# A DeltaNet and dilated-attention layer on one core: bias table from 128 partitions, new buffers for the second half, and last loads re-placed

## The chip, the core and the metric

The kernel runs on one core of a Trainium2 chip. The metric is the device time of one execution in microseconds; lower is better. Three executions of the kernel before took 1434.2, 1432.68 and 1436.26 us, with a median of 1434.2.

## The reference

One layer for a sequence of 2048 positions of width 1024, in float32:

```python
h = rms_norm(x, norm_w)
proj = h @ w_in                       # 1024 -> 4104 columns: q, k, v, z, b, a of DeltaNet; q, k, v, gate of attention
# gated DeltaNet: 4 heads of 128, chunks of 64
q, k, v = split(silu(causal_conv4(qkv_dn)));  q, k = l2_norm(q), l2_norm(k)
for each chunk:                       # u, w from a triangular solve within the chunk
    v_new = u - w @ S;  o = q_dec @ S + attn_intra @ v_new
    S = S * g_last + k_tail.T @ v_new
y_dn = rms_norm(o, dn_norm_w) * silu(z)
# attention: 8 heads of 64, three patterns (window, dilation) = (128,1), (512,4), (2048,16)
for each pattern:
    scores = q @ k_window.T + bias[t5_bucket(step * dilation)]   # causal band of 129 keys
    o_p, lse_p = softmax(scores) @ v_window, logsumexp(scores)
y_att = sum(softmax over patterns(lse_p) * o_p) * silu(gate)
out = x + concat(y_dn, y_att) @ w_out
```

## The kernel before

All products of the projections and of the output run as three TensorE matmuls on rounded parts (high by high, high by low, low by high), so every operand x, weight or mixed activation is first "split": ACT copies the high part (xh, wh, mhh), DVE subtracts to get the low part (xl, wl, mhl). The work falls into stages that PE runs through in this order.

1. Projections of DeltaNet's q, k, v with their convolution, of z and the gates, and the inverse of the 32x32 diagonal blocks of the triangular systems, which DVE computes row by row. This is some 450 us. Their end also builds the bias table: `pb` is one matmul of the 33 rows of `rel_bias` with a one-hot table, and lines 594 f. write it to memory as `bs_d`, 64 copies of a row of 256 values per head and pattern, so that attention can load it as a sheared band.
2. The delta rule, up to about 801 us. `stage2` (line 606) prepares four chunks of a pair of heads: it loads kT, qT, vT (transposed k, q and v), Qr, E (decays), TTz and D0t (parts of the triangular system) on SP's queue and makes at, Ks and U from them. `chain` runs the recurrence of a chunk. `dn_out` (line 741) loads the gate rows zs, norms and gates the result and stores it as `y_d`. A scheduler orders these three by priorities. Products of attention's projections (`proj_fill`, tile pj) fill PE between them: 960 are free to go, what is beyond is held until the delta rule's last PE operation.
3. Attention. From here on every instruction is issued as written: `Queue` (line 88) chains each engine's instructions in program order, and all of them show line 99. The outputs are in two halves of 1024 positions, each with four pairs of heads. A pair of heads takes 12 steps, so there are 96 (and a few before and behind). `step` calls `scores` (sc, scores of a unit; DVE adds the bias and takes the maximum ml, ACT the exponential pr), `turned` (pt, transposes of pr, copied to pT) and `values` (pv, the product with V), and between them takes filler matmuls: in steps -4 to 47 `proj_fill`, 9, 9 and 8 of them; in steps 48 to 97 `out_fill`, 4, 4 and 3.
4. `at_step` is the table that puts the rest into a step's three places (0, 1, 2): `load` (q, K and the bias of a pair, 4 steps ahead), `queries`, `keys`, `vload`, `sums`, `weigh` and `weigh2` (weights of the three patterns), `blend_load` (weights as Fb, gate as gt), `blend` (on POOL, one per quarter of the positions) and `mixed` (the store to `mx_d`).
5. `out_fill` computes out = x + mixed @ w_out in rows of 128 positions. A job is a row's "dn" half (yt, loaded from `y_d`, turned by PE) or its "att" half (mt, loaded from `mx_d`). `half_load` loads it, `half_split` splits it, `products` yields the matmuls (tile po), and res, loaded from x or from a partial sum, takes the result. w_out is split by `wo_split`: its first four blocks of 128 rows near the end of `proj_fill` (loads `w_out_load`, tile wraw), the other four inside `out_fill` (RAW).
6. Behind step 97 the last pair is weighed, blended on DVE and multiplied (`opening`, `closing`).

DMAs are issued from SP's queue unless the code says `adma` (ACT's). SP and ACT share eight completion lanes: a DMA waits for the DMA eight back on its lane.

Of the kernel before, what the change touches and what calls it, by code (L numbers as in the profile page):

```python
# [84 lines left out]
def hybrid(tc, xT, x, norm_w, w_in, conv_w, a_log, dt_bias, dn_norm_w, q_norm_w, k_norm_w,  # L85
# [53 lines left out]
    bs_d = dr.tile([8, 3, 64 * 256], F32, name="bs_d")  # L139
# [447 lines left out]
    bv = scr[:8, :768].rearrange("p (a b) -> p a b", a=3)  # L587
    for i in range(2):
        pb = psA.tile([P, 512], F32, name="pm", bufs=1)
        n = 512 - 256 * i  # L590
        nc.tensor.matmul(pb[:8, :n], rb, oh[:, i * 512:i * 512 + n], start=True, stop=True)
        nc.vector.tensor_copy(scr[:8, i * 512:i * 512 + n], pb[:8, :n])
# [13 lines left out]
    def stage2(pair, c0):  # L606
# [15 lines left out]
        for s_ in range(2):  # L622
            dma(Qr[:, :, s_], dap(rows_d, (12 + 2 * pair + s_) * S + c0 * CH, [[0, P], [CH, 4], [1, CH]]))
# [5 lines left out]
        dma(E, Es_d[hf][pair, cc:cc + 4].rearrange("u p i -> p u i"))  # L629
# [3 lines left out]
        for s_ in range(2):  # L633
            a = s_ * CH
            dma(TT[a:a + CH, :, a:a + CH], A_d[hf][pair, cc:cc + 4, a:a + CH].rearrange("u p i -> p u i"))
            dma(D0[a:a + 32], dap(D0_d[hf], (m0 + s_) * 1024, [[32, 32], [2048, 4], [1, 32]]))
# [66 lines left out]
        return dict(WQ=WQ, at=at_, Ks=Ks, U=U, o4=o4)  # L703
# [54 lines left out]

# [9 lines left out]
    G = {}  # L768
    for p_ in range(2):
        G[p_] = at_prio("prep", stage2, p_, 0)  # L770
    for c0 in range(0, 32, 4):
# [8 lines left out]
        for p_ in range(2):  # L780
            at_prio("out", dn_out, p_, c0, cur[p_])
# [83 lines left out]
    def wo_split(kt, raw):  # L865
        wh, wl = W[kt]
        if kt < 4:
            nc.scalar.mul(wh, raw, dnw)
            nc.vector.scalar_tensor_tensor(wl, raw, dnw, wh.bitcast(F32), op0=ALU.mult, op1=ALU.subtract)
# [11 lines left out]
    def w_out_load(k):  # L881
        r = wp.tile([P, 4, 260], F32, name="wraw", bufs=2).rearrange("p a b -> p (a b)")[:, :1024]
        dma(r, w_out[k * P:(k + 1) * P, :])
        return r

    def proj_fill():
# [5 lines left out]
        for s_ in range(12):  # L892
# [3 lines left out]
            for o8 in range(8):  # L896
# [70 lines left out]
    def heads(hf, p):  # L967
# [5 lines left out]
        def load():  # L973
            g["q1"] = at0.tile([P, 1024], F32, name="q1", bufs=QB)
            g["k1"] = KC[p % 2] if hf else K0[:, p % 2 * 1024:(p % 2 + 1) * 1024]
            dma(g["q1"], qkT_d[0][p][:, T0:T0 + 1024])
            dma(g["k1"], qkT_d[1][p][:, :1024 * (hf + 1)])
            g["bias"] = bias = at0.tile([P, 3, 192], F32, name="bias", bufs=2)
            for s_ in range(2):
                dma(bias[s_ * CH:(s_ + 1) * CH],  # L980
                    dap(bs_d, (2 * p + s_) * 3 * 64 * 256 + 63, [[255, CH], [64 * 256, 3], [1, 192]]))
# [222 lines left out]
        g.update(load=load, keys=keys, queries=queries, vload=vload, scores=scores, turned=turned, values=values,  # L1204
# [13 lines left out]
    G[0]["load"]()  # L1218
    take(gen, 2 * 192)
# [24 lines left out]
    for i, g in enumerate(G):  # L1244
        b = 12 * i
        if i:
            at_step(b - 4, 1, g["load"])
        at_step(b - (2 if i else 3), 1, g["queries"], 0)
# [11 lines left out]
        if i < 7:  # L1260
# [5 lines left out]
            for qd in range(4):  # L1266
                d = i < 6
                at_step(b + 16 + qd + d, 0 if d else 2, g["blend_load"], qd)
                at_step(b + 17 + qd + d, 0 if d else 1, g["blend"], qd, nc.gpsimd)
                at_step(b + 19 + qd + d, 0 if d else 1, g["mixed"], qd)  # L1270
# [254 lines left out]
```

## Time and profile before

| | us |
|---|---|
| median of three executions | 1434.2 (1432.68 to 1436.26) |
| profiled execution | 1434.53 |
| its span | 1432.6 |
| mean granted TensorE clock | 0.988 |
| PE busy | 1376.4, 10262 matmuls |
| DVE, ACT, POOL busy | 905.4, 677.1, 438.4 |
| DMA | 205.00 MB, mean 143 GB/s |

The span is from the first to the last instruction of the trace; the time of the execution has a little around it. "Busy" counts the time in which an engine has an instruction in work. The waits view lists for how long an engine stood idle and what came last before it went on. The windows view gives busy time, granted clock (PEclk, 1.00 is full speed) and the DMA engines' mean busy share for stretches of the span.

### The profile page before, as it was taken

The page shows a single profiled execution, that of the slowest core. Times are in us where ns is not written, and L with a number is a line of the kernel's source. Part 1 is how long each engine was busy: PE and PEld are TensorE (multiplying, and loading weights), DVE is VectorE, ACT ScalarE, POOL GpSimd, SP SyncE. Part 2 cuts the span into 40 slices and gives each one's busy share as a digit, 9 for nine tenths or more (in the row PEclk, how much of TensorE's full clock was granted, in tenths as well). Part 3 has the DMA queues.
Part 4 walks back from the last instruction along what each step waited for, and adds up shares of the span by engine and source line. Part 5 has one row for each costly group of instructions (what it writes and reads, how often), then busy time and mean ns, then how long its engine had stood idle before and what let it go on. Part 6 is the DMA issues. An engine that isn't in the chain of part 4 may idle for free.

```text
span 1432.6 us, 28797 instructions
## 1 busy us (share of the span) xinstructions
PE 1376.4 (96%) x10262; PEld 1224.8 (85%) x10262; DVE 905.4 (63%) x2787; ACT 677.1 (47%) x1929; POOL 438.4 (31%) x507
## 2 busy tenths in 40 slices
PE   8999999999999997999999899999998989999998
PEld 7998777777777797999999889999997778888877
DVE  7535668799995365777777664634444645556465
ACT  5634436652221333444444376666565545555520
POOL 3000000000002113442332523565675275665500
PEclk9999999999999999999999999999999999999999
DMA  6563446763648646557553555274657474765664
GB/s 192 179 111 83 101 89 136 150 121 84 116 77 176 171 80 165 134 147 193 129 147 77 114 132 137 76 190 98 147 135 235 138 253 135 220 169 158 194 191 142
DMA packets 301154, 205.00 MB, mean 143 GB/s; under 512 B 149283, under 2 KB 271027, under 8 KB 300500
## 3 DMA queue, kind: packets, MB, share of 16 engines
q1 hardware_dynamic: 233924, 171.70, 48.6%
q10 hardware_dynamic: 67088, 31.47, 8.0%
q8 instruction: 81, 1.33, 0.4%
q14 instruction: 61, 0.50, 0.1%
HBM read 142.61 MB, written 60.50 MB: 142 GB/s over the span
## 4 chain that ended last, share of the span: by engine, by line
PE 66%; DVE 14%; DMA 9%; ACT 4%; issue 4%; SPq 1%; POOL 1%; ACTq 0%; DVEq 0%; POOLq 0%
PE pj L99 15%; PE po L99 9%; PE sc L99 6%; PE pz L99 5%; PE pv L99 4%; PE pj L206 4%; PE pj L207 4%; PE pj L208 4%; PE pt L99 4%; DVE cy L478 3%; DVE inv L545 2%; DMA kT<-cv 2%; PE C L719 2%; PE SU L725 2%; DVE inv L547 2%
## 5 line engine op out<-in xcount | busy, mean ns | idle before, releaser
L99 ACT ACTIVATE pr<-pr,ml 128x192 f32<-128x192 f32 (+2 forms) x384 | 156.8, 409 | 168.7 <-DVE ml L99 156.9
L99 PE MATMUL pj<-wh,xh 128*128 128x256 f32 (+1 forms) x776 | 228.2, 294 | 3.6 <-DVE t L99 2.3
L99 PE MATMUL pj<-wl,xh 128*128 128x256 f32 (+1 forms) x776 | 226.6, 292 | 0.0
L99 PE MATMUL pj<-wh,xl 128*128 128x256 f32 (+1 forms) x776 | 224.9, 290 | 0.0
L208 PE MATMUL pj<-xh,wl 128*128 128x512 f32 x512 | 203.6, 398 | 3.2 <-DVE wl L192 3.2
L206 PE MATMUL pj<-xh,wh 128*128 128x512 f32 x512 | 203.8, 398 | 1.4 <-ACT cy L480 1.2
L207 PE MATMUL pj<-xl,wh 128*128 128x512 f32 x512 | 203.0, 396 | 0.0
L99 PEld LDWEIGHTS pj<-wh,xh 128*128 128x128 f32 x776 | 147.6, 190 | 4.3 <-DVE t L99 2.7
L99 PEld LDWEIGHTS pj<-wl,xh 128*128 128x128 f32 x776 | 148.0, 191 | 0.6 <-issue 0.4
L99 PEld LDWEIGHTS pj<-wh,xl 128*128 128x128 f32 x776 | 147.7, 190 | 0.2
L99 DVE CUSTOM_DVE_ANT_0 pr<-sc,bias 128x192 f32<-128x192 f32 (+2 forms) x384 | 100.3, 307 | 74.3 <-PE sc L99 73.4
L208 PEld LDWEIGHTS pj<-xh,wl 128*128 128x128 f32 x512 | 96.5, 188 | 26.6 <-DVE wl L192 4.5
L206 PEld LDWEIGHTS pj<-xh,wh 128*128 128x128 f32 x512 | 96.6, 189 | 24.8 <-ACT cy L480 1.6
L478 DVE SCALAR_TENSOR_TENSOR cy<-cu,cw,cy 128x512 f32<-128x512 f32 x144 | 107.6, 749 | 15.9 <-ACT cy L476 14.4
L207 PEld LDWEIGHTS pj<-xl,wh 128*128 128x128 f32 x512 | 96.5, 188 | 22.0
L99 POOL COPY qz<-q 64x512 f32<-64x512 f32 x96 | 94.5, 984 | 57.8 <-PE sc L99 53.9
L662 POOL MEMSET at__4536<- 64x256 f32 x1 | 0.3, 306 | 354.5 <-PE pj L207 354.5
L99 DVE COPY pT<-pt 64x128 f32<-64x128 f32 (+2 forms) x220 | 69.4, 323 | 60.1 <-PE pt L99 56.8
L99 PE MATMUL po<-xh,mhh 128*128 128x512 f32 x212 | 89.6, 422 | 2.5 <-ACT mhh L99 2.5
L99 POOL TENSOR_TENSOR Fb<-Fb,op 128x256 f32<-128x256 f32 x84 | 70.6, 854 | 60.8 <-DMA Fb<-F 59.7
L99 PE MATMUL po<-xl,mhh 128*128 128x512 f32 x212 | 88.6, 418 | 0.0
L99 PE MATMUL po<-xh,mhl 128*128 128x512 f32 x212 | 88.4, 417 | 0.0
(365 smaller groups left out, 3169.8 us busy)
## 6 DMA issues: line engine op xcount, KB each, us to landing
wraw<-in_w_in SPq DMA_DIRECT2D x44, 512.0 KB, 7.0
cv<-cy ACTq DMA_DIRECT2D x48, 256.0 KB, 2.6
Fb<-F SPq DMA_DIRECT2D x64, 192.0 KB, 5.8
xr<-in_xT SPq DMA_DIRECT2D x32, 256.0 KB, 4.1
kT<-cv SPq DMA_DIRECT2D x32, 256.0 KB, 3.3
qk<-qs ACTq DMA_DIRECT2D x64, 128.0 KB, 3.6
res<-in_x SPq DMA_DIRECT2D x13, 512.0 KB, 5.3
V<-v_d SPq DMA_DIRECT2D x20, 256.0 KB, 6.2
```

Of the source, the lines that this page charges most:

```text
L99: i = f(*args, **kw)
L206: nc.tensor.matmul(ps, wh[:, k, c * P:(c + 1) * P], xh[tb][:, kt, :], start=kt == 0, stop=False)
L207: nc.tensor.matmul(ps, wh[:, k, c * P:(c + 1) * P], xl[tb][:, kt, :], start=False, stop=False)
L208: nc.tensor.matmul(ps, wl[:, k, c * P:(c + 1) * P], xh[tb][:, kt, :], start=False, stop=kt == KT - 1)
L478: nc.vector.scalar_tensor_tensor(y, u[:, i:i + 512], cw[:, ct, i:i + 1], y, op0=ALU.mult, op1=ALU.add)
L545: nc.vector.tensor_tensor(pr_[:, :i, :i], Tt[:, :i, :i], L[:, None, :i, i].to_broadcast([P, i, i]), op=ALU.mult)
L547: nc.vector.tensor_reduce(Tt[:, :i, i], pr_[:, :i, :i], axis=AX.X, op=ALU.add)
L662: nc.gpsimd.memset(at_[:CH, :, :CH], 0.0)
L719: nc.tensor.matmul(pc[:, s_], g["WQ"][:, u, s_], S0[:, s_], start=True, stop=True)
L725: nc.tensor.matmul(su[:, s_], g["Ks"][:, u, s_], VN, start=True, stop=True)
```

## The change

- The bias table: the matmul's stationary operand holds each head's column 16 times (33x128 instead of 33x8), so the result has 128 rows. The three writes to `bs_d` leave 128 partitions, 4 copies of 256 values each, instead of 8 partitions with 64 copies; memory is laid out by pattern first. Each write is issued behind the zs loads of one of the first three groups of four chunks.
- The first two preparations of the delta rule issue E, TTz and D0t on ACT's queue. The first zs loads are put behind the second D0t, and the order of two small pool tiles ahead of it changes.
- Blocks 0, 1 and 2 of w_out are loaded together where 0 and 1 were; block 2 uses two "big" buffers and its split has two parts; block 3 is loaded with the split of block 0.
- `load` is cut in two: K has its own entry, `load_k`. In the first half it stays in the same place, now behind the bias; for the first pair of the second half it is 2/3 of a step later, for the next three 1 1/3 steps later.
- For the first six pairs the blendings are 4, 3 and 4 thirds of a step apart instead of 3, with their loads and stores.
- The second half: the buffers of its pool are laid out anew (mt, C1, yt, res, K1), the first job is split ahead of step 48 (`take(gen, 2)`), the loads of RAW are apart from each other and so are its four splits, and the parts h and l of a split activation are one tile mh.
- The last loads: mt of rows 8 and 13 goes into the bias's buffers, loads run four jobs ahead from product 20 on, the last `sums_back` is half on ACT's queue, and steps 84 to 90 take 10 filler matmuls instead of 11.


```diff
@@ bias table
-    bs_d = dr.tile([8, 3, 64 * 256], F32, name="bs_d")
+    bs_d = dr.tile([3, 8, 64 * 256], F32, name="bs_d")
...
-    for i in range(3):
-        dma(dap(bs_d, i * 64 * 256, [[3 * 64 * 256, 8], [256, 64], [1, 256]]),
-            bv[:, i, None, :].to_broadcast([8, 64, 256]))
+    def bias_out(i, after):
+        d = dma(dap(bs_d, i * 8 * 64 * 256, [[4 * 256, P], [256, 4], [1, 256]]),
+                bv[:, i, None, :].to_broadcast([P, 4, 256]))
+        tc.add_manual_dep(d.ins, after.ins.name, NOSYNC, reason="behind the loads of a group of chunks")
@@ stage2, dn_out, and the loop over groups of four chunks
-        dma(E, Es_d[hf][pair, cc:cc + 4].rearrange("u p i -> p u i"))
+        dma2(E, Es_d[hf][pair, cc:cc + 4].rearrange("u p i -> p u i"))
...
+            if c0 == 0:
+                tc.add_manual_dep(z.ins, last_D0[0].ins.name, NOSYNC, reason="behind the first preparations'")
...
-        G[p_] = at_prio("prep", stage2, p_, 0)
+        G[p_] = at_prio("prep", stage2, p_, 0, adma)
...
+        if c0 < 12:
+            at_prio("out", bias_out, c0 // 4, z)
@@ w_out: loads of its first half
     def w_out_load(k):
-        r = wp.tile([P, 4, 260], F32, name="wraw", bufs=2).rearrange("p a b -> p (a b)")[:, :1024]
-        dma(r, w_out[k * P:(k + 1) * P, :])
-        return r
+        if k == 2:
+            rs = [mid.tile([P, 512], F32, name="big", bufs=3) for _ in range(2)]
+        else:
+            rs = [wp.tile([P, 4, 260], F32, name="wraw", bufs=2).rearrange("p a b -> p (a b)")[:, :1024]]
...
-                        rs = [w_out_load(k) for k in range(2)]
+                        rs = [w_out_load(k) for k in range(3)]
...
-                        if o8 < 6:
-                            rs.append(w_out_load(o8 - 2))
+                        if o8 == 4:
+                            rs.append(w_out_load(3))
@@ attention: table of steps
             at_step(b - 4, 1, g["load"])
+            at_step(*((b - 4, 1) if i < 4 else (b - 3, 0) if i == 4 else (b - 3, 2)), g["load_k"])
...
-                at_step(b + 17 + qd + d, 0 if d else 1, g["blend"], qd, nc.gpsimd)
+                if i < 6:
+                    k = 3 * b + (54, 58, 61, 65)[qd]
+                    m = k + 6 + (i == 2 and qd == 3)
+                    at_step(*divmod(k - 3, 3), g["blend_load"], qd)
+                    at_step(*divmod(k, 3), g["blend"], qd, nc.gpsimd)
+                    at_step(*divmod(m, 3), g["mixed"], qd)
+                    at_step(*divmod(k + 12, 3), ready.add, (i // 4, i % 4, qd))
...
-            at_step(b + 13, 1, g["sums_back"], 1, dma)
+            at_step(b + 13, 1, g["sums_back"], 1, adma)
@@ second half: buffers, loads and splits
+            if tt in (8, 13):
+                t = at0.tile([P, 3, 192], F32, name="bias", bufs=2).rearrange("p a b -> p (a b)")[:, :512]
...
+    wo.tile([P, 512], F32, name="mt", bufs=2)
+    C1 = wo.tile([P, S], F32, name="C1")
+    loaded = {i: half_load(Q2[i], "dn", 4) for i in range(2)}
     RAW = [wo.tile([P, D], F32, name="res", bufs=3) for _ in range(2)]
-    C1 = wo.tile([P, S + 80], F32, name="C1")[:, :S]
-    loaded = {i: half_load(Q2[i], "dn", 4) for i in range(2)}
...
+        raws = {(0, 1): (raw_load, 0), (0, 2): (raw_load, 1), (0, 12): (raw_load, 2), (0, 22): (raw_load, 3)}
+        for k, at_ in enumerate(((0, 20), (1, 18), (2, 10), (3, 2))):
+            raws[at_] = (lambda k=k: wo_split(4 + k, RAW[k]),)
...
-                        load(i + 3 if nth < 24 else i + 5)
+                        load(i + 3 if nth < 20 else i + 4 if nth < 24 else i + 5)
...
+    take(gen, 2)
     for t in range(48, NST + 2):
-        step(t, gen, {48: (1, 1, 4)}.get(t, (4, 4, 3)))
+        step(t, gen, (4, 3, 3) if 84 <= t < 91 else (4, 4, 3))
```

The change moves instructions in three places of which the prediction speaks. The first is SP's queue in the delta rule, where the writes of the bias table (bs_d, read from the buffer K) stand among the loads of the preparations (kT, qT, vT, Qr, TTz, D0t, E) and the gate rows zs and stores y_d of the output; wraw is a weight for the filler. Before:

```order
L594 DMA bs_d<-K_4460 8x64x256
L635 DMA TTz_4474<-A_70 64x4x64 x2
L636 DMA D0t<-D_74 32x4x32 x2
L594 DMA bs_d<-K_4460 8x64x256 x2
L619 DMA qT<-cv_57 128x512
L629 DMA E_5100<-Es_72 128x4x64
L618 DMA kT<-cv_59 128x512
L620 DMA vT<-cv_62 128x512
L635 DMA TTz_4473<-A_70 64x4x64 x2
L636 DMA D0t<-D_74 32x4x32 x2
L623 DMA Qr<-rows_d 128x4x64 x2
L619 DMA qT<-cv_58 128x512
```

And after, the first of the three writes with what stands around it:

```order
L635 DMA E_5202<-Es_72 128x4x64
L764 DMA y_d<-o_4584 64x4x128 x2
L752 DMA zs<-zs_d 64x4x128 x2
L599 DMA bs_d<-K_4461 512x1x256
L624 DMA kT<-cv_60 128x512
L629 DMA Qr<-rows_d 128x4x64
L626 DMA vT<-cv_61 128x512
L629 DMA Qr<-rows_d 128x4x64
L641 DMA TTz_4473<-A_70 64x4x64 x2
L764 DMA y_d<-o_4686 64x4x128 x2
L752 DMA zs<-zs_d 64x4x128 x2
```

Before, the three writes stand ahead of the preparation's loads and in the midst of them; now each is alone, behind a pair of zs loads, and the other two follow 23 and 46 entries later, behind the next zs loads.

The second is PE at the switch to the second half, where pj is the last projection product (wh, wl the weight's parts, xh, xl the activation's), sc the scores, po<-cs,yt the transposes of the first output row, pt those of the weights pr, and po<-xh the output products. Before:

```order
L99 MATMUL pj<-wh,xh_9195 128x256
L99 MATMUL pj<-wl,xh_9195 128x256
L99 MATMUL pj<-wh,xl_9196 128x256
L99 MATMUL sc<-K_8198,qz_8741 128x192 x4
L99 MATMUL po<-cs,ml 96x128
L99 MATMUL pt<-cs,pr 128x128 x2
L99 MATMUL po<-cs,yt 128x128 x4
L99 MATMUL po<-xh_12389,mhh 128x512
L99 MATMUL po<-xl_12390,mhh 128x512
L99 MATMUL po<-xh_12389,mhl 128x512
```

And after:

```order
L99 MATMUL pj<-wh,xh_9197 128x256
L99 MATMUL pj<-wl,xh_9197 128x256
L99 MATMUL pj<-wh,xl_9198 128x256
L99 MATMUL po<-cs,yt 128x128 x4
L99 MATMUL sc<-K_8200,qz_8743 128x192 x4
L99 MATMUL po<-xh_12384,mh 128x512
L99 MATMUL po<-xl_12385,mh 128x512
L99 MATMUL po<-xh_12384,mh 128x512 x2
L99 MATMUL po<-cs,ml 96x128
L99 MATMUL pt<-cs,pr 128x128 x2
```

The first row's transposes are now ahead of the first scores, and its first four products follow the scores directly.

The third is SP's queue ahead of that switch: q, K and bias of the second half's first pair, wraw the blocks of w_out (big those of its third block), Fb and gt the loads of a blending, mx_d its store, V the values. Before:

```order
L99 DMA V<-v_d 64x4x128 x2
L99 DMA wraw<-in_w_out 128x1024
L99 DMA q_12396<-qk_76 128x1024
L99 DMA K_8198<-qk_80 128x2048
L99 DMA bias<-bs_d 64x3x192 x2
L99 DMA mx_d<-gt 128x256
L99 DMA wraw<-in_w_out 128x1024
L99 DMA mx_d<-gt 128x256
L99 DMA V<-v_d 64x4x128 x2
```

And after:

```order
L99 DMA wraw<-in_w_out 128x1024
L99 DMA q_12397<-qk_76 128x1024
L99 DMA bias<-bs_d 64x3x192 x2
L99 DMA Fb<-F_97 64x3x256 x2
L99 DMA gt<-gate_66 128x256
L99 DMA K_8200<-qk_80 128x2048
L99 DMA mx_d<-gt 128x256
L99 DMA V<-v_d 64x4x128 x2
L99 DMA mx_d<-gt 128x256
L99 DMA yt<-y_d 128x512 x3
```

One block of w_out is left where there were two (the third, as two big loads, is now 9 entries ahead of these); K stands behind the bias and one blending's loads, and three yt loads follow.

## Rows read from the trace of the kernel before

**Rows 1.** The page's first part: busy us, share of the span, instructions of each engine.

```profile
PE 1376.4 (96%) x10262; PEld 1224.8 (85%) x10262; DVE 905.4 (63%) x2787; ACT 677.1 (47%) x1929; POOL 438.4 (31%) x507
```

**Rows 2.** Waits of PE: what it waited for, us in total, times, longest.

```profile
PE A L680 <- DMA vT<-cv: 6.6, 1, 6.6
PE pv L99 <- DVE pT L99: 5.1, 2, 4.5
PE sc L99 <- DVE ml L99: 4.3, 3, 2.3
PE A L642 <- DMA D0t<-D: 4.2, 1, 4.2
PE pv L99 <- DVE res L99: 3.7, 1, 3.7
...
PE po L99 <- ACT mhh L99: 2.5, 2, 1.9
PE pj L99 <- DVE t L99: 2.3, 1, 2.3
PE A L699 <- ACT tmp L690: 1.8, 2, 1.0
PE po L99 <- DMA yt<-y_d: 1.8, 1, 1.8
```

**Rows 3.** Windows: us, PE, PEld, DVE, ACT, POOL busy, PEclk, DMA share, GB/s.

```profile
470.00:475.00 5.00, 5.00 (x25) 4.27 (x20) 1.42 (x4) 0.00 (x0) 0.57 (x1) 0.64 0.85 231
525.00:549.00 24.00, 17.79 (x179) 17.27 (x177) 15.02 (x48) 8.11 (x27) 6.84 (x10) 0.92 0.54 90
550.00:555.00 5.00, 5.00 (x37) 5.00 (x36) 0.00 (x0) 0.06 (x1) 2.03 (x4) 0.79 0.77 210
785.00:801.00 16.00, 12.66 (x86) 10.35 (x84) 14.03 (x47) 6.20 (x21) 2.03 (x3) 1.00 0.52 67
1015.00:1020.00 5.00, 3.72 (x23) 3.50 (x25) 1.95 (x10) 2.60 (x10) 3.63 (x7) 0.66 1.02 149
1080.00:1090.00 10.00, 6.63 (x60) 6.26 (x59) 2.44 (x12) 3.83 (x13) 4.18 (x6) 1.00 1.01 293
1090.00:1095.00 5.00, 3.90 (x23) 3.58 (x24) 2.83 (x12) 3.47 (x12) 0.00 (x0) 0.66 0.05 16
1100.00:1105.00 5.00, 4.64 (x14) 3.98 (x15) 1.91 (x9) 1.46 (x6) 2.46 (x3) 0.67 0.69 249
1130.00:1135.00 5.00, 5.00 (x45) 3.94 (x45) 4.23 (x14) 3.18 (x12) 0.00 (x0) 0.76 0.52 168
...
1170.00:1175.00 5.00, 5.00 (x20) 4.26 (x19) 1.99 (x7) 1.95 (x9) 0.59 (x1) 0.66 1.00 331
1380.00:1385.00 5.00, 5.00 (x20) 3.98 (x20) 3.73 (x10) 0.38 (x1) 0.00 (x0) 0.84 0.20 66
```

**Rows 4.** Timeline of SP's queue, delta rule: start us, us, issue.

```profile
512.11 0.29 SPq L594 DMA_DIRECT2D bs_d<-K  x1
...
538.28 4.06 SPq L620 DMA_DIRECT2D vT<-cv  x1
```

**Rows 5.** Timeline in attention, with idle time before and its releaser.

```profile
1075.61 0.34 SPq L99 DMA_DIRECT2D wraw<-in_w_out  x1
...
1087.94 1.15 ACT L99 ACTIVATE xh<-wraw,dnw 128x1024 fp32r<-128x1024 f32 x1 [4.56 <-DMA bias<-bs_d]
...
1168.16 0.69 DVE L99 TENSOR_TENSOR res<-po,res 128x512 f32<-128x512 f32 x1 [5.38 <-DMA res<-in_x]
...
1376.81 0.51 ACT L99 CAST mhh<-mt 128x384 fp32r<-128x384 f32 x1 [5.47 <-DMA mt<-mx_d]
```

**Rows 6.** Tile K in 1210 to 1245 us: duration ns, first and last start.

```profile
L99 PE MATMUL sc<-K,qz x16: 325/326/326, 1237.4 to 1242.9; 128*128 128x192 f32 x16
L99 SPq DMA_DIRECT2D K<-qk x1: 423/423/423, 1220.3 to 1220.3; - x1
...
DMA to landing us min/median/max: 10.0/10.0/10.0
```

More of the change, by code (lines that the diff above doesn't have):

```diff
@@ L569, in hybrid @@
             conv_proj(w, pair)
+    mid.tile([P, 512], F32, name="t0", bufs=2)
     rs0 = [mid.tile([P, 512], F32, name="big", bufs=3) for _ in range(2)]
@@ L604, in hybrid, with stage2 @@
     SU = psD.tile([P, 4, P], F32, name="SU", bufs=1)
-    def stage2(pair, c0):
+    def stage2(pair, c0, dma2=dma):
         hf, cc = divmod(c0, 16)
@@ L780, in hybrid @@
         for p_ in range(2):
-            at_prio("out", dn_out, p_, c0, cur[p_])
+            z = at_prio("out", dn_out, p_, c0, cur[p_])
+        if c0 < 12:
+            at_prio("out", bias_out, c0 // 4, z)
     close(psD_g)
@@ L867, in wo_split @@
         if kt < 4:
-            nc.scalar.mul(wh, raw, dnw)
-            nc.vector.scalar_tensor_tensor(wl, raw, dnw, wh.bitcast(F32), op0=ALU.mult, op1=ALU.subtract)
+            for i, r in enumerate(raw):
+                n = r.shape[1]
+                h, l = wh[:, i * n:(i + 1) * n], wl[:, i * n:(i + 1) * n]
+                nc.scalar.mul(h, r, dnw)
+                nc.vector.scalar_tensor_tensor(l, r, dnw, h.bitcast(F32), op0=ALU.mult, op1=ALU.subtract)
         else:
@@ L881, in w_out_load @@
     def w_out_load(k):
-        r = wp.tile([P, 4, 260], F32, name="wraw", bufs=2).rearrange("p a b -> p (a b)")[:, :1024]
-        dma(r, w_out[k * P:(k + 1) * P, :])
-        return r
+        if k == 2:
+            rs = [mid.tile([P, 512], F32, name="big", bufs=3) for _ in range(2)]
+        else:
+            rs = [wp.tile([P, 4, 260], F32, name="wraw", bufs=2).rearrange("p a b -> p (a b)")[:, :1024]]
+        n = D // len(rs)
+        for i, r in enumerate(rs):
+            dma(r, w_out[k * P:(k + 1) * P, i * n:(i + 1) * n])
+        return rs
     def proj_fill():
@@ L980, in load, with load_k @@
                 dma(bias[s_ * CH:(s_ + 1) * CH],
-                    dap(bs_d, (2 * p + s_) * 3 * 64 * 256 + 63, [[255, CH], [64 * 256, 3], [1, 192]]))
+                    dap(bs_d, (2 * p + s_) * 64 * 256 + 63, [[255, CH], [8 * 64 * 256, 3], [1, 192]]))
+        def load_k():
+            g["k1"] = KC[p % 2] if hf else K0[:, p % 2 * 1024:(p % 2 + 1) * 1024]
+            dma(g["k1"], qkT_d[1][p][:, :1024 * (hf + 1)])
             g["kc"] = {0: g["k1"].rearrange("p (c i) -> p c i", c=1)}
@@ L1202, in mixed @@
             dma(mx_d[p, :, T0 + qd * 256:T0 + (qd + 1) * 256], g["gt", qd])
-        g.update(load=load, keys=keys, queries=queries, vload=vload, scores=scores, turned=turned, values=values,
+        g.update(load=load, load_k=load_k, keys=keys, queries=queries, vload=vload, scores=scores, turned=turned, values=values,
                  sums=sums, sums_out=sums_out, sums_back=sums_back, weigh=weigh, weigh2=weigh2, factors=factors, blend_load=blend_load, blend=blend,
@@ L1312, in ring_mh @@
     def ring_mh():
-        return [wo.tile([P, 4, P], F32R, name="mh" + c, bufs=3) for c in "hl"]
+        t = wo.tile([P, 2, 4, P], F32R, name="mh", bufs=3)
+        return [t[:, 0], t[:, 1]]
     def res_load(tt, src, res=None):
@@ L1325, in half_load @@
         else:
-            t = wo.tile([P, 512], F32, name="mt", bufs=2).rearrange("p (k c) -> p k c", k=4)
+            if tt in (8, 13):
+                t = at0.tile([P, 3, 192], F32, name="bias", bufs=2).rearrange("p a b -> p (a b)")[:, :512]
+            else:
+                t = wo.tile([P, 512], F32, name="mt", bufs=2)
+            t = t.rearrange("p (k c) -> p k c", k=4)
             dma(t[:, :n], mx_d[:n, :, tt * P:(tt + 1) * P].rearrange("k p c -> p k c"))
@@ L1389, in split @@
                 if buf not in spare:
-                    t = wo.tile([P, S + (80 if buf == "C1" else 48)], F32R, name=buf)[:, :S]
+                    t = wo.tile([P, S + (0 if buf == "C1" else 150)], F32R, name=buf)[:, :S]
                     t = t.rearrange("p (a b k c) -> p a b k c", a=2, b=2, k=4)
@@ L1397, in split, with raw_load @@
             return ops
-        for k in range(4):
+        def raw_load(k):
             dma(RAW[k], w_out[(4 + k) * P:(5 + k) * P, :])
@@ L1426, in out_fill @@
                     m += 1
-                    if nth < 2 and m in (8, 16):
-                        k = 2 * nth + m // 8 - 1
-                        wo_split(4 + k, RAW[k])
+                    if (nth, m) in raws:
+                        f, *args = raws.pop((nth, m))
+                        f(*args)
                     if m >= 3 * n and m % 3 == 0 and todo_:
```

35 lines of the change are left out of this document (20 added, 15 removed).

## Prediction

> **What bounds the kernel now.** I read the shares of busy time first [rows 1]: PE is busy for 1376.4 us of a span of 1432.6, 96%, and the next engine, DVE, 63%. So time can come from two places alone: the 56.2 us in which PE stands still, and stretches where its granted clock is at the lower of its two levels (1.2 instead of 2.4 GHz). Second, the waits of PE by releaser [rows 2]: a few of them are single long stops (6.6 on vT, 4.5 on pT, 4.2 on D0t, 3.7 on res), not many short ones. Third, windows of 5 us behind each long stop [rows 3]. After every one of them the clock has fallen: .64 in 470–475, .79 in 550–555, .66 in 1015–1020, .66 in 1090–1095, .67 in 1100–1105, .76 in 1130–1135, .66 in 1170–1175, .84 in 1380–1385. At a mean clock c a window of 5 us does 5c of work at full speed, so it loses 5(1−c): 1.8, 1.05, 1.7, 1.7, 1.65, 1.2, 1.7 and 0.8 us. A stop therefore costs its wait and this loss. Last I asked for what released each stop: DMA issues of SP in the delta stage [rows 4], the waits of ACT and DVE in attention [rows 5], and the lead of a K load [rows 6].
>
> The stops with both terms, in us: first preparation 4.2 + 1.8 = 6.0; vT 6.6 + 1.0 (the stop on tmp) + 1.05 = 8.7; 1016 2.3 + 1.7 = 4.0; 1091 4.5 + 1.7 = 6.2; 1097 1.8 (yt) + 0.6 (mhh) + 1.65 = 4.1; 1128 2.3 + 1.2 = 3.5; 1169 3.7 + 1.7 = 5.4; 1377 1.9 + 0.8 = 2.7. Sum 40.6. The change touches what stands ahead of each of them.
>
> **The change part by part.** The profiled execution took 1434.53 us, 1.9 beyond its span and 0.3 above the median of 1434.2; gains are taken from 1434.5.
>
> *Bias table.* Before, three writes of 0.52 MB each leave 8 partitions; SP issues the first at 512.11, the others after it, and only at 538.28 vT's load [rows 4], for which PE waits 6.6. In 525–549 the DMA engines are busy to .54, and move 90 GB/s [rows 3], while 1170–1175 shows that 1.00 and 331 GB/s can be had: half of the engines carry the writes and everything else stands behind them. After, each write leaves 128 partitions, one for each of three groups of four chunks, behind that group's gate loads. At 90 GB/s, or at twice that, 0.52 MB takes 5.8 or 2.9 us, and vT no longer stands behind two of them. Nearest row for the length: a load of 1 MB lands in 10.0 us [rows 6], so half of one in about 5.0. Gain: 8.7 at most; 2.9 if the write that now stands just ahead of the next kT delays that load by a full 5.8 with PE waiting. I take 8, since kT is asked for well ahead of its products. The added matmul columns are none (the output has 128 rows instead of 8, the same 768 columns), and the one added copy of 33x128 on DVE lies ahead of the delta stage, where DVE waits anyway; free.
>
> The .54 share has a name. The Trainium skill, page "DMA: Bandwidth & Descriptors", section "Why a DMA increments its semaphore by 16 and not by 1", says that a transfer is split over the largest number of engines, up to 16, that divides the slowest dimension of both sides: 8 for 8 partitions, 16 for 128. The row's half share agrees with it. By that rule alone each write is twice as fast, and the whole of 8.7 would come back.
>
> *First preparations.* E, TTz and D0t of the first two preparations move from SP to ACT's queue, and zs goes behind them. Before, PE stops 4.2 us for D0t [rows 2], the last of a row of loads on SP. The DMA engines are busy to .85 still at 470–475 [rows 3], and PE now comes to these products 14 projection matmuls earlier; 25 fill 5 us there, so 14 are 2.8 us of lost cover. I take 0, with ends at −2.8 (loads no earlier) and +6.0 (the stop goes).
>
> Here a rule speaks against the change. The Trainium skill, same page, section "Issuing engines are not separate DMA queues": transfers that ACT issues run on the same 16 engines as SP's and interleave with them, and a second issuer saves only issue time. By it this edit gives 0; by the wait that the row shows, 6.0. I went with 0 from the busy DMA engines.
>
> *Delta stage's end.* In 785–801 PE is busy for 12.66 of 16 us and DVE for 14.03 [rows 3]; the projection matmuls that fill gaps have run out. The new order has them two chain steps longer: +1, from −1 to +2.
>
> *Blendings (1016).* POOL works 3.63 of 5 us there, and DVE's product t waits for POOL's ss, then PE for t. After, the four blendings of a group start 4, 3, 4 thirds of a step apart instead of 3, so ss comes in between. It can also collide elsewhere: +2.5, from 0 to 4.0.
>
> *w_out and K around 1091.* SP issues w_out's third block at 1075.61, and ACT's split of it starts at 1087.94, 12.3 us later, after 4.56 us idle [rows 5]; ACT is in order, so pr and then pT and PE stand behind it. In 1080–1090 the DMA engines are full (1.01, 293 GB/s). After, blocks 0 to 2 are asked for together, a whole group of products earlier, and K of the second half (1 MB) goes behind the bias. K's first reader is still 2 or more steps off. +5.8; ends 3 (if the fourth block is late, at half the price) and 6.2.
>
> *Switch to the second half (1097).* Before, yt is loaded into memory that the last projection matmuls still read, so its load waits for them. After, the pools are laid out so that it need not, and PE has yt's transposes ahead of the scores. yt is then early, but its split onto ACT and DVE stands ahead of pr there: +2.5, from −2 (pr and pT late by what ACT and DVE take for the split) to 4.1.
>
> *Splits of w_out's second half (1128).* Four splits at fixed products become four further apart; +2, from 0 to 3.5.
>
> *res ahead of K (1169).* DVE waited 5.38 us for res [rows 5], issued behind q, a 1 MB K and the bias, at a full 331 GB/s. Now K goes after res: +4, from 0 (the same bytes, another transfer is last) to 5.4.
>
> *Last loads (1377).* ACT idles 5.47 us for mt [rows 5]; more buffers, earlier loads: +1.5, from 0 to 2.7.
>
> *New waits.* Every load that moves earlier displaces another: −3, from −10 to 0.
>
> Sum: 8 + 0 + 1 + 2.5 + 5.8 + 2.5 + 2 + 4 + 1.5 − 3 = 24.3, and 1434.5 − 24.3 = 1410.2; on the median's footing 1410.
>
> **The rivals.**
>
> *DMA bound in attention.* The bytes do not change, and full windows (1.00 to 1.02) stand at 1015, 1080 and 1170. If the queue decides, the waits at 1016, 1097, 1128, 1169 and 1377 come back under other names, and only vT (8.0) and 1091 (5.8, where the load moves into a free stretch) are gained: 1434.5 − 13.8 = 1420.7. Against it: behind 1091 the share is .05, so that there is room within microseconds.
>
> *K comes late.* Before, K is issued at 1220.3, 3 2/3 steps ahead of its first reader, lands in 10.0 us, and is read by PE at 1237.4 [rows 6]: 17.1 us of lead, a slack of 7.1. The change issues it 1 1/3 steps later for the last three pairs of heads (2/3 for the one at the switch), so 2 1/3 of 3 2/3 are left, 10.9 us, and a slack of 0.9. Landing in 12.3 us, as w_out's block took at 1075, makes it 1.4 late. Each late K stops PE for the lateness and 1.7 of clock, at three places; that eats the 24.3 from 6.4 us of lateness each (24.3 / 3 − 1.7), a landing of 17.3. Should K land in twice 10.0, it is 9.1 late, 32.4 in all, and the time is 1410.2 + 32.4 = 1442.6. For it: by this count the slack is gone, and a K behind res in a full stretch may well take longer. Against: it would have to land 7.3 us later than the one of before.
>
> *The table still stalls.* Its bytes are the same and in pieces of the same length (256 floats); if the piece, not the number of partitions, sets the rate, the group's loads stand behind it thrice, and 8 is not gained: 1434.5 − 16.3 = 1418.
>
> **How the numbers follow.** Forecast .67, DMA bound .20, table .06, K late .07. 1410 is the first's, with a range of its own of 1401 to 1419. The range over the cases reaches up to the DMA bound with some of its spread, 1425, and down to 1397, the sum with first preparation (6.0), 1097 and 1128 at their good ends and no new waits (24.3 + 6.0 + 1.6 + 1.5 + 3 = 36.4, so 1398, rounded down for the terms not stretched). What can be told from no change is 0.3%, 4.3 us. Faster by more than that takes all of the forecast, the table's case and nearly all of the DMA bound: .89; same .05, from the DMA bound's and K's edges; slower .06, K late.
>
> **What would show it.** vT's wait gone and the three table writes apart, with the share above .54 about them; no ACT wait on wraw of 4 us near 1088; no DVE wait on res; no clock of .66 behind those places; PE's idle time some 35 us instead of 56. I am wrong if PE has waits on K's scores (sc) after each of the steps where a pair of heads begins, if a wait of over 3 us stands at the first preparation or the switch as before and new ones beside it, or if the idle time shrinks and the time does not.

## The result, and the profile after

The changed kernel took 1419.2 us (median of 6 executions, 1417.33 to 1425.79) against 1433.44 us for the kernel before (6 executions, 1430.92 to 1436.26). The ratio is 0.9909, 95% interval 0.9883 to 0.9936: 0.6 to 1.2% faster, some 13 us (14.2 between the medians) where 24.3 were forecast. The profiled execution took 1417.45 us, its span is 1415.7 us.

The page's first part after, to be set beside [rows 1]:

```profile
PE 1368.9 (97%) x10262; PEld 1218.4 (86%) x10262; DVE 905.4 (64%) x2789; ACT 675.1 (48%) x1930; POOL 437.3 (31%) x507
```

PE's idle time fell from 56.2 to 46.8 us, not to 35. Its busy time fell by 7.5 us for the same 10262 matmuls, while the mean granted clock rose from 0.988 to 0.995. What PE waits for after (us in total, times, longest):

```profile
PE sc L99 <- DVE ml L99: 5.8, 5, 3.3
PE A L648 <- DMA D0t<-D: 3.9, 1, 3.9
...
PE sc L99 <- POOL qz L99: 2.9, 2, 1.9
...
PE pv L99 <- DVE pT L99: 2.2, 2, 1.6
...
PE pj L99 <- DVE t L99: 1.4, 1, 1.4
...
PE po L99 <- DMA yt<-y_d: 0.9, 1, 0.9
```

Against [rows 2], the stop on vT is gone, as is PE's own wait on res; the one on D0t is as it was (4.2 before, 3.9 after); pT went from 4.5 to 1.6, t from 2.3 to 1.4, yt from 1.8 to 0.9. Two are new: 3.3 on ml and 1.9 on qz. The first stands behind DVE's wait for res, which is still there (f2 below). The windows that answer to [rows 3] (us; busy and number for PE, PEld, DVE, ACT, POOL; granted clock; DMA share; GB/s):

```profile
468.00:473.00 5.00, 5.00 (x31) 3.96 (x31) 1.42 (x4) 1.15 (x2) 1.19 (x3) 0.66 0.74 198
525.00:549.00 24.00, 24.00 (x235) 23.68 (x234) 18.36 (x59) 11.78 (x40) 13.45 (x20) 1.00 0.44 115
748.00:753.00 5.00, 5.00 (x32) 5.00 (x31) 4.12 (x11) 2.20 (x7) 1.83 (x2) 0.66 0.17 55
781.00:797.00 16.00, 12.62 (x91) 10.81 (x90) 13.21 (x41) 5.37 (x20) 3.21 (x4) 1.00 0.61 71
945.00:955.00 10.00, 8.05 (x73) 7.55 (x72) 4.12 (x18) 5.62 (x21) 9.54 (x11) 1.00 0.21 62
1150.00:1160.00 10.00, 6.68 (x56) 5.16 (x55) 3.80 (x20) 4.77 (x20) 8.04 (x11) 0.83 1.07 377
```

525 to 549 is now filled: 24.00 busy instead of 17.79. The reader is to see as well that 781 to 797, the delta stage's end, is as empty as before (12.62 of 16), and that 945 to 955, where PE never stood still before, has 1.95 us of idle time in it.

To see where the gain is lost, I took from each trace the time at which PE starts its n-th scores product (sc); attention has 816 of them in the same order in every kernel. Differences of two such times give a stretch's length. The kernels with the old attention (before, e1, e2, e3 below) and those with the new one (after, e4, f1, f2, f3, f4) are several traces of nearly the same code, so that chance shows too:

| stretch, at the time of before | old attention: before, e1, e2, e3 | new: after, e4, f1, f2, f3, f4 | gain, forecast |
|---|---|---|---|
| 942 to 986 (products 176 to 240) | 43.9 in all | 46.2, 48.0, 44.1, 49.5, 44.1, 43.0 | part of −3 |
| 1009 to 1023 (to 288) | 14.1, 12.4, 14.0, 15.2 | 10.0, 10.0, 13.0, 10.0, 9.8, 9.8 | 2.5 |
| 1080 to 1121 (368 to 416) | 41.4, 40.1, 39.3, 40.7 | 36.4, 36.5, 39.9, 37.0, 36.9, 37.6 | 5.8 + 2.5 |
| 1121 to 1136 (to 432) | 15.2, 14.9, 15.0, 14.9 | 11.9, 11.9, 11.5, 12.0, 11.9, 11.5 | 2 |
| 1158 to 1183 (464 to 496) | 25.1, 26.2, 22.8, 25.0 | 24.2, 23.7, 26.1, 23.7, 23.5, 21.2 | 4 |
| 1301 to 1398 (672 to 768) | 97.6, 96.4, 97.0, 96.0 | 93.3, 92.4, 94.0, 93.9, 92.7, 95.3 | 1.5 |

Two of these rows hold moved work as well as stops. Steps 84 to 90 take seven output products less, and they are not done at the end but at the switch, where the stretch from product 384 to 392 has 11 of them instead of 4. So of the 3.2 us that the last row shows in the mean, 2.0 lie in 672 to 728 and are work that went elsewhere; and the stretch from 1080 on has some 1.6 us more to do (7 products, 0.23 us apart).

One trace is one execution, and it need not be the median: the profiled executions of e2, e4, f2 and f3 are the fastest of their kernels, by 4.0 to 5.7 us, and that of g3 below is the slowest, by 6.0.

And ahead of attention, the first scores product itself, before and after (start us, us, ...):

```profile
814.02 1.26 PE L99 MATMUL sc<-K,qz 128*128 128x64 f32 x8
```

```profile
809.53 1.26 PE L99 MATMUL sc<-K,qz 128*128 128x64 f32 x8
```

After starts attention 4.5 us earlier. At 550, behind vT's place, it had been 8.5 earlier (the 65th product of D0t and TTz starts at 549.95 instead of 558.43). f1 and f2, which are the same code up to there, start attention at 805.7 and 803.6, so one trace of this stage stands for itself only within some 6 us.

### The profile page after: what moved, and what is told of

Same layout as the page of the kernel before. It is cut to its first block, busy times and chain, and to the rows that moved or that the text cites. A ratio compares the mean times of both kernels' runs of the same rounds, so it can differ in the third digit from the quotient of the medians.

```text
span 1415.7 us, 28800 instructions
## 1 busy us (share of the span) xinstructions
PE 1368.9 (97%) x10262; PEld 1218.4 (86%) x10262; DVE 905.4 (64%) x2789; ACT 675.1 (48%) x1930; POOL 437.3 (31%) x507
## 4 chain that ended last, share of the span: by engine, by line
PE 59%; DVE 15%; DMA 12%; ACT 4%; issue 4%; POOL 3%; SPq 2%; ACTq 0%; DVEq 0%; POOLq 0%
PE pj L99 12%; PE po L99 8%; PE pz L99 6%; PE sc L99 5%; PE pj L207 4%; PE pj L206 4%; PE pj L208 4%; PE pt L99 3%; PE pv L99 3%; DVE cy L478 3%; DVE inv L545 2%; POOL Fb L99 2%; PE C L725 2%; PE SU L731 2%; DMA Fb<-F 2%
## 5 line engine op out<-in xcount | busy, mean ns | idle before, releaser
L99 PE MATMUL po<-xh,mh 128*128 128x512 f32 x424 | 148.2, 413 | 0.4 <-DVE mh L99 0.4
L99 PEld LDWEIGHTS po<-xh,mh 128*128 128x128 f32 x424 | 78.3, 189 | 12.8 <-DVE mh L99 0.8
L99 PE MATMUL po<-xl,mh 128*128 128x512 f32 x212 | 87.0, 410 | 0.0
```

The costliest lines, as they stand in the source:

```text
L99: i = f(*args, **kw)
```

## The experiments

**e1, e2, e3, e4: the bias table.** Four kernels: the whole edit of the table alone on the kernel before; its 128 partitions alone; its places alone; and the changed kernel without it.

```diff
# e2, on the kernel before (e1 has bias_out and its call as well)
-        dma(dap(bs_d, i * 64 * 256, [[3 * 64 * 256, 8], [256, 64], [1, 256]]),
-            bv[:, i, None, :].to_broadcast([8, 64, 256]))
+        dma(dap(bs_d, i * 8 * 64 * 256, [[4 * 256, P], [256, 4], [1, 256]]),
+            bv[:, i, None, :].to_broadcast([P, 4, 256]))
# e3, on the kernel before: the 8-partition write within bias_out
+        if c0 < 12:
+            at_prio("out", bias_out, c0 // 4, z)
```

e1, expected: 

> The kernel before with the whole edit of the bias table (128 partitions and one write behind each of three groups' gate loads) and nothing else. Theory: the stop of 6.64 us on vT and the lower clock behind it go, PE reaches the preparation behind it 8 to 9 us earlier, and the first scores of attention 4.5 to 8.5 us earlier; time 1425 to 1429. Rival: the delta stage gives the gain back by its end whatever else is changed, since small stops of PE on DVE and ACT come in; then the first scores come at most 5 us earlier, and the time is 1428 to 1430.

e2, expected: 

> The kernel before with the writes of the bias table from 128 partitions, all three still issued where they were. Theory (the number of partitions is what counts): each write lands in about 3 to 6 us instead of trickling for 25, the DMA engines are busy well above .54 in 525 to 549, the stop on vT is below 2 us, time 1425 to 1427. Rival (the place counts, since 1.57 MB in pieces of 1 KB stand ahead of the preparation's loads either way): vT still stops PE for 4 us or more, time 1431 to 1434.

e3, expected: 

> The kernel before with the writes of the bias table from 8 partitions as before, but one behind each of three groups' gate loads. Theory (partitions): each write keeps half of the DMA engines for 6 to 12 us, and the loads behind it are late three times, by 2 to 4 us; time 1429 to 1434. Rival (the place): one write at a time is covered by the preparation's lead, the stop on vT goes, time 1425 to 1427.

e4, expected: 

> The changed kernel with the bias table as before. Theory: the stop of 6 to 7 us on vT near 543 to 549 comes back with its clock, time 8 to 10 us above the changed kernel, 1427 to 1429. Rival (given back by the delta stage's end): only 4 to 5 us above it, 1423 to 1424.

Measured, each with its ratio to the kernel before (1432.84): e1 1430.99, 0.999 (0.9977 to 1.0003); e2 1430.09, 0.9984 (0.9964 to 1.0005); e3 1450.49, 1.0131 (1.0107 to 1.0155); e4 1424.85, 0.9962 (0.994 to 0.9983).

In e1 and e2 the stop on vT is gone; in both, the stretch of [rows 3] is full (24.00 of 24). In e2:

```profile
525.00:549.00 24.00, 24.00 (x233) 23.52 (x232) 18.13 (x56) 11.34 (x37) 12.77 (x19) 1.00 0.37 99
```

So the number of partitions does it, with no help from the places: e2's writes land in 3.3 to 5.0 us each, those of e1 and of the changed kernel in 3.8 to 5.9, while a write from 8 partitions that is alone, as in e3, takes 12.3 to 12.7. In the trace the semaphore that tells of a write's landing is raised by 8 landings for a write from 8 partitions, and by 16 for one from 128. The rule that the prediction cited (the Trainium skill, "DMA: Bandwidth & Descriptors", "Why a DMA increments its semaphore by 16 and not by 1") agrees in the 8 and the 16; by it alone a write would take half the time, and here it takes a quarter to a half. The DMA share about the writes is .93 in e2 (512.8 to 522.2), and .74 to .89 in the changed kernel.

The slow writes also held up the issuing. In the kernel before, SP's issues of qT, E, kT and vT between 525 and 542 take 4.1 to 4.7 us each, where the median of its 860 issues is 0.45, so vT's load is not even issued until 538.28 [rows 4]; in e3 the issue of vT behind the first write takes 4.1 again. In e2 it goes out 12 us earlier:

```profile
526.28 0.32 SPq L622 DMA_DIRECT2D vT<-cv  x1
```

Of the expectations, e2's mechanism came out but not its time: 1430.1 lies between the ranges of theory and rival. The places alone are harmful: e3 took 1450, far above both of its ranges. One write from 8 partitions at a time still takes over 12 us to land, and each stands ahead of a preparation's loads, so that three stretches of 30 us lose 6.0, 3.7 and 7.4 us of PE's time, and the clock beside it:

```profile
545.00:575.00 30.00, 23.97 (x203) 23.28 (x202) 16.78 (x53) 9.72 (x35) 7.32 (x10) 0.83 0.61 133
592.00:622.00 30.00, 26.27 (x224) 25.71 (x223) 17.48 (x54) 11.07 (x35) 6.58 (x7) 0.89 0.57 132
636.00:666.00 30.00, 22.59 (x195) 21.95 (x194) 15.67 (x50) 9.54 (x31) 4.69 (x5) 0.83 0.63 144
```

But e1's time fell by 2 us, not by 9, and its interval does not tell these 2 us from none. At the 65th product of D0t and TTz it is 9.6 us ahead of before, at its first scores 2.1. The rival of e1 holds in this, though its time, 1428 to 1430, is just missed. So does the rival of e4, with 1423 to 1424 expected and 1424.85 measured. The stage's end in e1, then in before:

```profile
777.00:799.00 22.00, 14.24 (x87) 12.34 (x85) 16.32 (x55) 5.99 (x25) 3.13 (x4) 0.84 0.38 59
```

```profile
777.00:801.00 24.00, 20.66 (x156) 18.35 (x154) 21.12 (x68) 10.80 (x37) 4.84 (x6) 1.00 0.53 83
```

Both have 1008 projection products to fill gaps with until the delta rule is over. In before the last of them is done with 28 of the 256 state products (SU) to go, in e1 with 32: the last eight steps of the chain run bare, and PE waits for DVE step by step (7.8 us idle, clock .84; in before 3.3 us). From the last filler product to the chain's end e1 takes 23.0 us, before 13.7. A stop that goes does not make the chain shorter; the filler is only used up earlier. In e4 the first scores start at 814.0, as in before, and in the three traces of the changed kernel's delta stage at 803.6 to 809.5; there the order lets the filler last until 20 products are left.

**f3, g1, h1: more filler in the delta stage.** If that is the reason, more filler must bring the gain back. A filler product takes some 0.11 us, 36 of them 4.0.

```diff
-                        if n == HOLD * 192:
+                        if n == HOLD * 192 + 36:
...
-    take(gen, 2 * 192)
+    take(gen, 2 * 192 + 36)
...
-        step(t, gen, (8, 8, 8) if t < 0 else (9, 9, 8))
+        step(t, gen, (8, 8, 8) if t < 0 else (9, 8, 8) if t < 36 else (9, 9, 8))
```

f3 (on the changed kernel), expected: 

> The changed kernel with 36 more of attention's projection products free to go in the delta stage (1044 instead of 1008 before its last PE operation), and one fewer in each of 36 steps of attention. Theory (the table's gain is given back since the filler runs out 20 chain products before the end): the products cover the last chain steps, PE's idle time behind 786 falls from 4.8 us to below 2, the first scores come where they were although 36 products more are done, time 1415 to 1417. Rival (the chain itself is late, or the steps of attention have too few products between their scores and what waits on them): no gain or a loss, 1418 to 1423.

g1 (on e1), expected: 

> The kernel before with the bias table's edit and with 36 more projection products free to go in the delta stage (1044), one fewer in each of 36 steps of attention; the rest as before. With the table alone it was 1431.0. Theory (the table's 9 us are given back since the filler runs out 32 chain products before the end: 7.8 us of idle PE and 3.4 us at the lower clock's cost there): time 1424 to 1427, idle PE behind 777 halved. Rival (the chain of the delta rule ends no earlier, whatever fills it): 1430 to 1432.

Measured: f3 1413.19 (1407.47 to 1414.97), ratio 0.9853 (0.9828 to 0.9878), where the changed kernel has 0.9909; g1 1424.02, ratio 0.994 (0.9919 to 0.996), where e1 has 0.999. Both intervals lie clear of those without the filler, f3's by little; f3 is even below its theory's range, which ended at 1415. The stage's end of g1, then of f3:

```profile
777.00:799.00 22.00, 18.00 (x127) 16.31 (x126) 15.61 (x55) 5.95 (x24) 3.82 (x4) 0.92 0.38 63
```

```profile
781.00:797.00 16.00, 13.92 (x112) 13.02 (x112) 12.13 (x39) 4.97 (x19) 2.84 (x3) 1.00 0.44 64
```

g1 starts attention at 810.6 (e1 811.9) with 36 products more behind it, so at equal work it is 5.3 us ahead of e1. So e1's trace shows where the table's gain went, into an end of the stage without filler, and g1 bears it out. The kernel before with more filler and the old table was not run, so how much of g1's 7 us it would have gained by itself stays open; its end had 3.3 us idle. For f3 the place of the gain is not shown: by the same count f3 and f4, the same code up to there, reach attention at 803.6 and 808.7, against 803.6 to 809.5 without the filler, and in f3's trace part of the gain lies in attention's first steps.

h1 has 64 more of them, and f1's edit below.

```diff
+                        if n == HOLD * 192 + 64:
...
+    take(gen, 2 * 192 + 64)
...
+        step(t, gen, (8, 8, 8) if t < 16 else (9, 8, 8))
```

Expected: 

> The changed kernel with 64 more projection products free to go in the delta stage (1072), fewer in attention's first steps, and the fourth blending's loads a third of a step earlier. Theory (filler covers the last chain products, and the stop on qz near 951 does not come): 1408 to 1413, the fastest so far or as fast as with 36. Rival (with 36 the end was covered, the rest only takes cover from attention's steps): 1414 to 1418.

Measured: 1411.65 (1410.98 to 1420.06), ratio 0.987 (0.9842 to 0.9897), which is the same as f3 within the intervals, so 64 bring no more than 36. Both are faster than the kernel before. Of the two, f3's interval lies just clear of the changed kernel's, and h1's overlaps it.

**f1: the new stop at 951.** In the changed kernel POOL's fourth blending comes late and holds up a copy of q (qz) that PE needs:

```profile
944.17 1.56 POOL L99 TENSOR_TENSOR Fb<-Fb,op 128x256 f32<-128x256 f32 x2 [7.69 <-DMA Fb<-F]
...
951.11 1.20 PE L99 MATMUL sc<-K,qz 128*128 128x64 f32 x7 [1.95 <-POOL qz L99]
```

```diff
-                    at_step(*divmod(k - 3, 3), g["blend_load"], qd)
+                    at_step(*divmod(k - 3 - (qd == 3), 3), g["blend_load"], qd)
```

Expected: 

> The changed kernel with the fourth blending's loads (Fb, gt) of each of the first six pairs a third of a step earlier, so that they are issued ahead of the q, bias and K of the pair two further on. Theory: the new stop of 1.95 us on qz at 951 is a POOL blending that waited 7.69 us for that Fb; it goes, the 3.8 us that the changed kernel loses between 935 and 951 come back, time 1415 to 1417. Rival (the DMA engines, .98 busy there, are the bound): V or K lands later instead, PE waits as long on them, time as the changed kernel's 1419.

Measured: 1417.1, ratio 0.9887 (0.9862 to 0.9911). The stop went: PE has no wait on qz there in f1, f4 and h1, which have the edit, and one of 0.9 to 3.7 us in after, e4, f2, f3 and g3, which do not. In the table's first row f1 has 44.1 and f4 43.0, against 46.2, 48.0 and 49.5 in after, e4 and f2; f3, with the shortest of these stops, has 44.1 too. So the load had slipped behind q, bias and K of a later pair. Of those 2 to 5 us the time shows 2.1, and the two intervals overlap; f1's trace loses as much again in 1080 to 1121, and 3 us in 1009 to 1023.

**f2: res half a job earlier.** The change put res ahead of K, and DVE still waits 5.15 us for it (5.38 in [rows 5]), with PE behind:

```profile
1152.71 0.69 DVE L99 TENSOR_TENSOR res<-po,res 128x512 f32<-128x512 f32 x1 [5.15 <-DMA res<-in_x]
...
1153.87 1.67 PE L99 MATMUL sc<-C,qz 128*128 128x128 f32 x8 [3.32 <-DVE ml L99]
```

```diff
-                res = RES[tt] if kind == "att" else res_load(tt, x)
+                res = RES[tt] if kind == "att" else early.pop(tt, None) or res_load(tt, x)
...
+                    if nth >= 3 and m == 3 * n + 2 and todo0 is not None and jobs[todo0][1] == "dn" and jobs[todo0][3][0]:
+                        early[jobs[todo0][0]] = res_load(jobs[todo0][0], x)
```

Expected: 

> The changed kernel with the res row of an output job loaded half a job earlier (from the fourth job on), ahead of q, bias and Fb. Theory: DVE's wait of 5.15 us for res near 1152, PE's 3.32 behind it and the lower clock (1.7) go, time 1414 to 1416. Rival (DMA bound): q, mt or V is late by as much at the same place, time 1418 to 1420.

Measured: 1419.29, ratio 0.9905 (0.9882 to 0.9927): no change. The wait on res is gone, and PE waits for V in its place:

```profile
1140.60 1.09 PE L99 MATMUL pv<-pT,V 128*64 128x128 f32 x16 [1.71 <-DMA V<-v_d]
...
1152.92 0.69 PE L99 MATMUL pv<-pT,V 128*64 128x64 f32 x16 [2.26 <-DMA V<-v_d]
```

f4, which has the edit too, takes 21.2 in the table's fifth row, but 23.6 instead of 22.0 in the stretch ahead of it. Here the rival, a DMA queue that is full whatever stands first in it, is borne out (share 1.07 in 1150 to 1160 above).

**f4: f1, f2 and f3 together.** Expected: 

> The three edits together on the changed kernel. Theory (three stops of their own): 1406 to 1411. Rival (what is gained at one place is given back at the next): 1414 to 1419.

Measured: 1413.13, ratio 0.9859 (0.9835 to 0.9883), as f3 alone, and between the ranges of theory and rival. f1's and f2's edits add nothing to it that can be seen.

**g2, g3: what ACT waits for at 1088.** The forecast read [rows 5] as a split that waits for its block of w_out. The rows ahead of it in the kernel before, on ACT and its queue, tell another story:

```profile
1082.57 0.81 ACT L99 ACTIVATE t<-pj,rstd 128x256 f32<-128x256 f32 x2
1087.52 0.38 ACTq L99 DMA_DIRECT2D v_d<-t  x1
```

t is done at 1083.4. ACT's own store of it goes out 4.1 us later, and the program makes that store wait for the completion lane that the bias load holds; the releaser in [rows 5] is named so ("<-DMA bias<-bs_d"). The block itself, issued at 1075.61, had landed 4.0 us later, at 1079.6; the fourth block, issued at 1080.72, took 9.2:

```profile
L99 SPq DMA_DIRECT2D wraw<-in_w_out x2: 339/340/342, 1075.6 to 1080.7; - x2
...
DMA to landing us min/median/max: 4.0/6.6/9.2
```

So the stores of q, k and v were moved to SP's queue:

```diff
-            adma(qkT_d[w][2 * g2 + j][:, tt * P:(tt + 2) * P], qs[:, j].rearrange("p a b -> p (a b)"))
+            dma(qkT_d[w][2 * g2 + j][:, tt * P:(tt + 2) * P], qs[:, j].rearrange("p a b -> p (a b)"))
...
-        adma(dap(v_d, tt * P * 512 + g2 * 256, [[512, P], [P * 512, 2], [1, 256]]),
+        dma(dap(v_d, tt * P * 512 + g2 * 256, [[512, P], [P * 512, 2], [1, 256]]),
```

g2 (on the kernel before), expected: 

> The kernel before with the stores of attention's q, k and v (qk, v_d) issued from SP's queue instead of ACT's. Theory: what ACT waited for near 1087 (4.56 us) and 1012 (3.72) was not w_out's block but its own store, held for a completion lane by the bias and K loads; with the store on SP both waits of ACT go, and PE's stop of 3 to 4.5 us on pT near 1084 to 1091, time 1426 to 1429. Rival (ACT waits for the block of w_out, as forecast): ACT idles there as before, time 1431 to 1434; or SP, waiting for the products itself, brings its loads late, 1435 and above.

g3 (on f3), expected: 

> The changed kernel with 36 more projection products in the delta stage and with the stores of q, k and v from SP's queue. Theory (stops of their own): ACT's waits of 5.65 near 936 and 2.0 near 1080 go with PE's stops behind them, 1407 to 1411, below the 1413.2 with the filler alone. Rival (SP's loads come late behind the stores): 1414 to 1420.

Measured: g2 1433.8, ratio 1.0012 (0.9994 to 1.003); g3 1419.72, ratio 0.9917 (0.9885 to 0.995), worse than f3 and in its rival's range: PE waits 4.9 us for yt at the switch there. In g2 ACT no longer waits for a store, but the time did not fall to the theory's 1426 to 1429. ACT now waits 2.32 us for the fourth block of w_out, a wait that the store had hidden:

```profile
1086.31 1.15 ACT L99 ACTIVATE xh<-wraw,dnw 128x1024 fp32r<-128x1024 f32 x1 [2.32 <-DMA wraw<-in_w_out]
...
1091.27 0.48 PE L99 MATMUL pt<-cs,pr 128*128 128x128 f32 x1 [2.39 <-DVE pT L99]
1093.37 1.09 PE L99 MATMUL po<-cs,yt 128*128 128x128 f32 x4 [1.63 <-DMA yt<-y_d]
```

PE's 16 scores products up to the switch take 10.2 us instead of 14.0 to 15.7, so the stop that the forecast priced is nearly gone (0.4 us of it left); the next 16 take 19.7 instead of 12.2 to 13.9, since SP now waits for the products whose stores it issues, and yt comes later yet. So the store was the first wait, the fourth block the second, and the yt load the third at one place. That ACT's stop near 1012 was of this kind too did not matter to PE: without it PE still waits there 2.2 us for t, behind POOL.

## Why the prediction was right, and where its sum was not

The direction and the range held, and so did the mechanism in part: time came from single long stops and the clock behind them. The size was 13 us where 24.3 were forecast, and 1419.2 is at the upper edge of the forecast's own 1401 to 1419. That it lies in the wide range of 1397 to 1425 is in part luck: three terms worth 17.8 us (bias table, w_out, res) gave much less, others somewhat more. The time cannot tell the cases apart either, since the DMA-bound rival's 1420.7 and the 1418 of "the table still stalls" are both nearer to it than 1410; the traces do. By the steps of the prediction:

- **Bias table, 8.** Right at its place: 8.5 us in the profiled pair, the stop and its clock gone, and by the number of partitions (e2). The rival that the table still stalls is refuted by the same traces. Wrong in the sum: alone it is worth 2 us at most (e1), since the filler then ends earlier (g1, with more filler, is 7 us faster). In company with the other edits it is worth more: e4, without it, is 5.6 us slower than the changed kernel. The prediction named the empty end [rows 3] and gave it +1; it should have asked what is late next.
- **First preparations, 0.** Held: 4.2 before, 3.9 after, and clocks of .64 and .66. That ACT's queue brings nothing where the DMA engines are busy (.85 before, .74 after) agrees with the Trainium skill's rule in "DMA: Bandwidth & Descriptors", section "Issuing engines are not separate DMA queues", as far as one wait can show it.
- **Blendings, 2.5.** 10.0 instead of 12.4 to 15.2 in five traces of six, some 3.5; mis-sized a little. That the new spacing does it is only likely: g1, with the old spacing, has 10.0 and no stop there, and f1, with the new, 13.0, since ACT waits 7.3 us for a store's lane. It brought the stop at 951 with it, 2 to 5 us in a trace: the forecast's "new waits" (−3), with a cause of its own (f1).
- **w_out and the switch, 5.8 + 2.5.** The failed step. It said that ACT's split waits for w_out's block, so that an earlier load sets ACT free. ACT's wait was for its own store, behind a lane that the bias load held. In the changed kernel (and f1) the lane is an Fb (or q) load's, and a wait of 2.0 (2.7) us is left. The 12.3 us, which the K rival uses as a landing time, were the split's delay; the block landed in 4.0. The stretch 1080 to 1121 gives 3.0 (mean 40.4 to 37.4), not 8.3. Cut at the switch, its first half, where ACT's stop lies, goes from 14.6 to 14.2, though with the first row's transposes now in it; the second goes from 25.8 to 23.2 with seven more output products, so the switch gave its 2.5 and more. PE's stop on pT was also over-sized by one trace: 4.5 in before, but 3.2, 3.1 and 3.3 in e1, e2 and e3, with the same code there. In the new attention it is 1.6 or 1.7 in three traces and 3.0 or 3.1 in three.
- **Splits, 2.** 3.2 (15.0 to 11.8).
- **res ahead of K, 4.** Failed: 24.8 to 24.4 in the four traces of the table without f2's edit, and 24.9 and 27.2 in g3 and h1. Another transfer is late (f2). This is the DMA-bound rival at one place. It does not hold elsewhere: 1016, the switch, 1128 and 1377 have gains.
- **Last loads, 1.5.** 3.2 from 1301 on (mean 96.8 to 93.6), but 2.0 of them are the seven products that moved to the switch. What is left, 1.1 in 728 to 768, is near the forecast.
- **K late.** Did not occur: no wait of PE for K stands in the trace after.
- **The signs.** vT's wait is gone, with the share above .54 about the writes, and ACT's wait near 1088 is down to 2.0 us. But DVE's wait for res, lower clocks (.66 in 468 to 473 and in 748 to 753, .83 in 1150 to 1160) and 46.8 us of idle time instead of 35 are there. One sign of being wrong came up by its words: 3.9 us at the first preparation as before, and new waits (3.3, 1.9) beside it. The forecast itself had put the first at 0 gain and the second at −3.

By stretches the profiled pair differs by 16.9 us (1432.6 to 1415.7), the medians by 14.2; with the spread of some 6 us of the delta stage the rest can't be told apart.

## What to carry to other kernels

A stop that is removed is worth its length only until the next place where the engines meet (e1: 9.6 us at the stop, 2.1 at the stage's end); where filler with a fixed quota covers a chain, ask when the filler ends after the edit, and move the quota with it. Where an engine that also issues DMAs stands idle, look at its queue's rows first: a store that waits for a lane stops all that is behind it, and the releaser's name, here a bias load, says so though the row's operands name something else. In the one stretch with full DMA engines that was tried (f2), putting one load ahead of another only renamed the wait. Before pricing a wait for a load, compare the load's landing with the time at which its reader starts.

## What the runs showed that I had not expected

Three kernels with the same code up to attention reached it at 803.6, 805.7 and 809.5 us. Part of the difference is in stops of about 1 us in the delta stage, one of which (1.25 us at 746) is followed by the lower clock in the changed kernel's trace (.66 in 748 to 753), while f1 and f2, with 1.06 and 0.97 us there, keep the full clock (1.00 in 740 to 757). In e3 the places that help nothing by themselves cost 17.7 us, because a write from 8 partitions in front of each group's loads is three stops where there had been one.
